# Add and gelu over two 1024x4096 arrays: halves of 64 KB rows become three contiguous blocks of 16, 53 and 59 KB rows

## The chip, the cores and the metric

The kernel runs on one core of a Trainium2 chip. The metric is device time in microseconds (us). Before the change the median of three runs is 120.08 us (120.03 to 120.22). About 0.24 us, 0.2% of that, is what a measurement of this kernel can tell from no change.

## The reference

Two float32 arrays of 1024x4096 go in, one comes out, element by element:

```python
z = x + y
out = 0.5 * z * (1 + np.tanh(np.sqrt(2 / np.pi) * (z + 0.044715 * z ** 3)))
```

Each array has 16.78 MB, so 33.55 MB are read and 16.78 MB written.

## The kernel before

Every array is seen as 128 rows, one for each partition: `xv`, `yv` and `ov` (L87) give partition p the p-th stretch of 32,768 contiguous elements, 128 KB. The kernel works on the two halves of these rows, 64 KB per partition each. The tile `zt` (L117, 128 KB per partition) holds all of x, then z, then the result, in place. The tile `yt` (L118, 64 KB per partition) holds one half of y at a time, so the second half of y can only be loaded when the adds of the first half have read the first.

All transfers are issued by SP, in this order: the first half of y (`load_y`, L128), the first and the second half of x (`load_x`, L123), then the second half of y in two pieces of 12,288 and 4,096 columns (48 and 16 KB per partition), then two stores of 64 KB per partition (`store`, L132). The y piece of 12,288 columns waits for the first six adds, the piece of 4,096 columns for the next two.

VectorE adds in place, `z = z + y`, in pieces of 2,048 columns (`add`, L151; the last two have 1,024). ScalarE follows with the gelu in place (`gelu`, L156). GpSimd takes no part in it (`by_pool` is empty), and no piece goes through PSUM (`in_psum` is empty).

The first store has a wait written by hand (L133 to L139): it isn't issued before add number 8, the first add of the second half, is done (`GATE = 8`).

Two helpers edit the finished program. `begin_early` (L11) moves SP's first two transfers ahead of the barrier at the start. `wait_late` (L23) takes the wait for the last store out of the common end and gives it to ScalarE. A small activation on the tile `one` loads the gelu table while the first loads run (L182, L183).

Of the kernel before, what the change touches and what calls it, by code (L numbers as in the profile page):

```python
# [8 lines left out]
def begin_early(nc, count):  # L9


    head, body = (b.instructions for b in nc.main_func.blocks[:2])
    SP = mybir.EngineType.SP
    moved = [i for i in body if i.engine == SP and isinstance(i, mybir.InstDMACopy)][:count]
    assert not any(i.sync_info and i.sync_info.on_wait for i in moved)
    assert all(i.regs_accessed() == ((), ()) for i in moved)
    at = next(k for k, i in enumerate(head) if i.engine == SP)
    for k, i in enumerate(moved):
        body.remove(i)
        head.insert(at + k, i)  # L20


def wait_late(nc):  # L23

    body, end = (b.instructions for b in nc.main_func.blocks[1:3])
    last = [i for i in body if isinstance(i, mybir.InstDMACopy)][-1]
    (sem,) = [u.id for u in last.sync_info.on_update]
    all_done = end[0]  # L30
    reset = next(i for i in end if isinstance(i, mybir.InstDrain) and i.is_reset_sema)
    at = end.index(reset)
    clear = end[at + 1]
    first, stop = reset.reset_range_start, reset.reset_range_stop
    assert all_done.engine == mybir.EngineType.SP and reset.engine == mybir.EngineType.Pool
    assert isinstance(clear, mybir.InstISA) and clear.engine == mybir.EngineType.Pool
    waits = all_done.sync_info.on_wait
    (its,) = [w for w in waits if w.id == sem]

    end[0] = mybir.InstDrain(  # L40
        name=all_done.name, engine=all_done.engine, debug=all_done.debug, is_reset_sema=False,
        sync_info=mybir.SyncInfo(on_wait=[w for w in waits if w.id != sem], on_update=[]),
    )
    parts = []
    for f, e in ((first, sem), (sem + 1, stop)):
        if f < e:
            nc.gpsimd.sem_clear(range(f, e))
            parts.append(nc.cur_bb.bb.instructions.pop())
    end[at + 1 : at + 2] = parts
    end.append(  # L50
        mybir.InstEventSemaphore(
            name=clear.name, engine=mybir.EngineType.Activation, debug=clear.debug,
            sync_info=mybir.SyncInfo(
                on_wait=[its],
                on_update=[
                    mybir.SyncUpdate(
                        sync_type="semaphore", id=sem, ant_name=its.ant_name,
                        update_mode="sem-sub-imm", update_value=its.wait_value,
                    )
                ],  # L60
            ),
        )
    )


@with_exitstack
def kernel(
    ctx: ExitStack,
    tc: tile.TileContext,
    x: bass.AP,  # L70
    y: bass.AP,
    out: bass.AP,
):

    nc = tc.nc
    P = nc.NUM_PARTITIONS  # L80
    fp32 = mybir.dt.float32
    act = mybir.ActivationFunctionType

    N, D = x.shape
    assert N % P == 0
    TOT = N // P * D
    xv, yv, ov = (a.rearrange("(p n) d -> p (n d)", p=P) for a in (x, y, out))  # L87

    HALF = TOT // 2
    xloads = [HALF, HALF]  # L90
    yloads = [16384, 12288, 4096]
    stores = [16384, 16384]
    chunks = [2048] * 15 + [1024, 1024]
    by_pool = []
    in_psum = []
    GATE = 8

    def ranges(sizes):
        ends = [sum(sizes[: i + 1]) for i in range(len(sizes))]
        assert ends[-1] == TOT  # L100
        return [(e - f, e) for e, f in zip(ends, sizes)]

    xr, yr, sr, cr = (ranges(r) for r in (xloads, yloads, stores, chunks))
    C = len(cr)
    second = next(c for c in range(C) if cr[c][0] == HALF)

    def over(rs, lo, hi):
        return [i for i, (a, b) in enumerate(rs) if a < hi and b > lo]

    pool_sb = ctx.enter_context(tc.tile_pool(name="xz", bufs=1))  # L110
    pool_y = ctx.enter_context(tc.tile_pool(name="y", bufs=1))
    pool_ps = ctx.enter_context(
        tc.tile_pool(name="ps", bufs=max(1, len(in_psum)), space=bass.MemoryType.PSUM)
    )

    one = pool_sb.tile([P, 992], fp32, tag="one", name="one")
    zt = pool_sb.tile([P, TOT], fp32, tag="z", name="z")  # L117
    yt = pool_y.tile([P, HALF], fp32, tag="y", name="y")  # L118
    xp, adds = {}, {}

    def load_x(i):
        a, b = xr[i]
        nc.sync.dma_start(out=zt[:, a:b], in_=xv[:, a:b])  # L123

    def load_y(i):
        a, b = yr[i]
        o = a % HALF
        nc.sync.dma_start(out=yt[:, o : o + b - a], in_=yv[:, a:b])  # L128

    def store(i):  # L130
        a, b = sr[i]
        ins = nc.sync.dma_start(out=ov[:, a:b], in_=zt[:, a:b])  # L132
        if i == 0 and GATE is not None:  # L133
            tc.add_manual_dep(
                ins.ins,
                adds[GATE].name,
                mybir.DependencyInfo(mybir.DependencyClass.Sync, mybir.DependencyReason.DATA),
                reason="the stores join the queue when the last load is nearly done",
            )  # L139

    def to_psum(c):
        a, b = cr[c]
        xp[c] = pool_ps.tile([P, 2048], fp32, tag="xp", name=f"xp{c}")
        nc.scalar.copy(out=xp[c][:, : b - a], in_=zt[:, a:b])

    def add(c):
        a, b = cr[c]
        o = a % HALF
        eng = nc.gpsimd if c in by_pool else nc.vector
        first = xp[c][:, : b - a] if c in in_psum else zt[:, a:b]  # L150
        ins = eng.tensor_add(out=zt[:, a:b], in0=first, in1=yt[:, o : o + b - a])  # L151
        adds[c] = ins.ins

    def gelu(c):
        a, b = cr[c]
        nc.scalar.activation(out=zt[:, a:b], in_=zt[:, a:b], func=act.Gelu_apprx_tanh)  # L156

    sp = [(load_y, i) for i in over(yr, 0, HALF)] + [(load_x, 0), (load_x, 1)]
    sp += [(load_y, i) for i in over(yr, HALF, TOT)]
    sp += [(store, i) for i in range(len(stores))]  # L160
    pool = [(add, c) for c in by_pool]
    dve = [(add, c) for c in range(C) if c not in by_pool]
    order = list(range(second, C))
    acts = [(gelu, c) for c in range(second)] + [(to_psum, c) for c in in_psum]
    acts += [(gelu, c) for c in order]
    assert sorted(order) == list(range(second, C))

    needs = {
        load_x: lambda i: [],
        load_y: lambda i: [(add, c) for c in over(cr, yr[i][0] - HALF, yr[i][1] - HALF)],  # L170
        to_psum: lambda c: [(load_x, i) for i in over(xr, *cr[c])],
        add: lambda c: [(load_x, i) for i in over(xr, *cr[c])]
        + [(load_y, i) for i in over(yr, *cr[c])]
        + [(to_psum, k) for k in in_psum if k == c],
        gelu: lambda c: [(add, c)],
        store: lambda i: [(gelu, c) for c in over(cr, *sr[i])]
        + ([(add, GATE)] if GATE is not None else []),
    }
    queues = [sp, pool, acts, dve]
    done = set()  # L180
    with tc.manual_schedule():
        nc.vector.memset(one[:, :1], 0.0)  # L182
        nc.scalar.activation(out=one[:, :1], in_=one[:, :1], func=act.Gelu_apprx_tanh)  # L183
        while any(queues):
            moved = False
            for q in queues:
                while q and all(n in done for n in needs[q[0][0]](q[0][1])):
                    fn, arg = q.pop(0)
                    fn(arg)
                    done.add((fn, arg))  # L190
                    moved = True
                    if q is not sp:
                        break
            assert moved, [q[:1] for q in queues]

    ctx.close()
    tc.close()
    tc.compile()  # L198
    begin_early(nc, 2)
    wait_late(nc)  # L200
# [30 lines left out]
```

## Time and profile before

| | |
|---|---|
| Median of three runs | 120.08 us (120.03 to 120.22) |
| The profiled execution's own time | 120.19 us |
| Its span, from the first to the last instruction | 118.70 us |
| VectorE busy | 35.5 us, 30% of the span |
| ScalarE busy | 32.0 us, 27% |
| DMA queue of SP | 1008 packets, 50.33 MB, 98.5% of 16 engines' span |

The span is what the profile's views cover; 1.49 us of the profiled execution lie outside it. In the views, a line such as L151 is a line of the kernel, "SPq" is SP's sequencer, which issues the transfers, and a transfer's "landing" is the last of its 16 completion signals. Beside the views, the trace has a record of each DMA packet with its start, its length and its bytes. Here each packet is one partition's row of one transfer (640 of 65,536 bytes, 128 of 49,152 and 128 of 16,384), and each transfer ends with 16 packets of 4 bytes, one on each of the 16 DMA engines. In the view of stretches of time, a packet is counted in the stretch where it starts, so a short stretch can show more than is possible and the next one less.

### The profile page before, as it was taken

The page shows a single profiled execution, that of the slowest core. Times are in us where ns is not written, and L with a number is a line of the kernel's source. Part 1 is how long each engine was busy: PE and PEld are TensorE (multiplying, and loading weights), DVE is VectorE, ACT ScalarE, POOL GpSimd, SP SyncE. Part 2 cuts the span into 40 slices and gives each one's busy share as a digit, 9 for nine tenths or more (in the row PEclk, how much of TensorE's full clock was granted, in tenths as well). Part 3 has the DMA queues.
Part 4 walks back from the last instruction along what each step waited for, and adds up shares of the span by engine and source line. Part 5 has one row for each costly group of instructions (what it writes and reads, how often), then busy time and mean ns, then how long its engine had stood idle before and what let it go on. Part 6 is the DMA issues. An engine that isn't in the chain of part 4 may idle for free.

```text
span 118.7 us, 96 instructions
## 1 busy us (share of the span) xinstructions
DVE 35.5 (30%) x18; ACT 32.0 (27%) x19; POOL 0.2 (0%) x4
## 2 busy tenths in 40 slices
DVE  0000000000000099999900000699999300000000
ACT  5000000000000029899850000079989800000000
POOL 0000000000000000000000000000000000000000
DMA  9889888998899888988898996998899889988890
GB/s 353 353 353 685 375 353 353 596 464 353 353 442 618 353 353 353 685 375 353 353 530 381 414 530 271 431 624 353 353 596 464 353 353 442 618 353 353 353 685 22
DMA packets 1008, 50.33 MB, mean 424 GB/s; under 512 B 112, under 2 KB 112, under 8 KB 112
## 3 DMA queue, kind: packets, MB, share of 16 engines
q1 hardware_dynamic: 1008, 50.33, 98.5%
HBM read 33.55 MB, written 16.78 MB: 424 GB/s over the span
## 4 chain that ended last, share of the span: by engine, by line
DMA 52%; DVE 22%; ACT 2%; DVEq 2%; ACTq 1%; SPq 0%; issue 0%
DMA z<-in_x_dram 34%; DVE z L151 22%; DMA y<-in_y_dram 17%; ACT z L156 2%; DVEq L198 2%; ACTq L198 1%; SPq L128 0%; DVEq L151 0%
## 5 line engine op out<-in xcount | busy, mean ns | idle before, releaser
L151 DVE TENSOR_TENSOR z<-z,y 128x2048 f32<-128x2048 f32 (+1 forms) x17 | 35.5, 2160 | 56.2 <-DMA z<-in_x_dram 40.0
L156 ACT ACTIVATE z<-z 128x2048 f32<-128x2048 f32 (+1 forms) x17 | 30.5, 1807 | 61.3 <-DVE z L151 61.3
L183 ACT ACT_TABLE_LOAD x1 | 1.3, 1283 | 1.3 <-PEq L215 1.3
L182 DVE MEMSET one<- 128x1 f32 x1 | 0.1, 59 | 1.3 <-PEq L215 1.3
L183 ACT ACTIVATE one<-one 128x1 f32<-128x1 f32 x1 | 0.2, 203 | 0.0
L215 POOL MEMSET const-bfloat16-1.0<- 128x1 bf16 x1 | 0.1, 101 | 0.0
L215 POOL MEMSET const-uint8-127<- 128x1 uint8 x1 | 0.1, 101 | 0.0
L215 POOL MEMSET const-float32-0.0<- 128x1 f32 x1 | 0.1, 98 | 0.2 <-issue 0.2
L215 POOL MEMSET const-float32-1.0<- 128x1 f32 x1 | 0.1, 98 | 0.0
## 6 DMA issues: line engine op xcount, KB each, us to landing
y<-in_y_dram SPq DMA_DIRECT2D x1, 6144.0 KB, 20.5
y<-in_y_dram SPq DMA_DIRECT2D x1, 2048.0 KB, 20.9
z<-in_x_dram SPq DMA_DIRECT2D x2, 50.1
out_dram<-z SPq DMA_DIRECT2D x2, 22.9
y<-in_y_dram SPq DMA_DIRECT2D x1, 22.0
```

Source lines behind the costliest of these rows:

```text
L151: ins = eng.tensor_add(out=zt[:, a:b], in0=first, in1=yt[:, o : o + b - a])
L156: nc.scalar.activation(out=zt[:, a:b], in_=zt[:, a:b], func=act.Gelu_apprx_tanh)
L182: nc.vector.memset(one[:, :1], 0.0)
L183: nc.scalar.activation(out=one[:, :1], in_=one[:, :1], func=act.Gelu_apprx_tanh)
L198: tc.compile()
L215: nc = _bacc.Bacc("TRN2", target_bir_lowering=False, num_devices=1)
```

## The change

The arrays are no longer seen as 128 rows of 128 KB. They are taken flat and cut into three blocks that lie one after the other in memory, and each block is cut into 128 rows: block 0 has rows of 4,096 elements (16 KB), block 1 of 13,568 (53 KB), block 2 of 15,104 (59 KB). Row p of a block goes to partition p.

- Loads: y's block 0, y's block 1, x's block 1, y's block 2, x's block 2, x's block 0: six instead of five. Stores: block 1, block 2, block 0: three instead of two.
- y's block 1 is loaded into the place of `zt` where x's block 2 goes later. So x's block 2 waits for all adds of block 1. y's blocks 2 and 0 have a place of their own in `yt`, which grows from 64 to 75 KB per partition.
- Compute: block 1 in pieces of 2,048 columns x6 and 1,280; block 2 in pieces of 2,816 and 2,048 x6; block 0 in two of 2,048.
- The hand-written wait of the first store is on the first add of block 2, the one of 2,816 columns.
- The two helpers stay; the transfers that now go ahead of the barrier are y's block 0 and y's block 1.

```diff
-    xv, yv, ov = (a.rearrange("(p n) d -> p (n d)", p=P) for a in (x, y, out))
+    PIECES = [[2048, 2048], [2048] * 6 + [1280], [2816] + [2048] * 6]
+    LEN = [sum(p) for p in PIECES]
+    GATE = (2, 0)
+    AT = [sum(LEN[:k]) for k in range(3)]
-    HALF = TOT // 2
-    xloads = [HALF, HALF]
-    yloads = [16384, 12288, 4096]
-    stores = [16384, 16384]
-    chunks = [2048] * 15 + [1024, 1024]
-    GATE = 8
+    def rows(a, k):
+        flat = a.rearrange("n d -> (n d)")
+        return flat[P * AT[k] : P * (AT[k] + LEN[k])].rearrange("(p c) -> p c", p=P)
...
+    zt = pool_sb.tile([P, TOT], fp32, tag="z", name="z")
+    yt = pool_sb.tile([P, LEN[2] + LEN[0]], fp32, tag="y", name="y")
+    def z(k, lo=0, hi=None):
+        return zt[:, AT[k] + lo : AT[k] + (LEN[k] if hi is None else hi)]
+    def y_at(k, lo=0, hi=None):
+        hi = LEN[k] if hi is None else hi
+        if k == 1:
+            return z(2, lo, hi)
+        o = 0 if k == 2 else LEN[2]
+        return yt[:, o + lo : o + hi]
+    def load_x(k):
+        nc.sync.dma_start(out=z(k), in_=rows(x, k))
+    def load_y(k):
+        nc.sync.dma_start(out=y_at(k), in_=rows(y, k))
+    def store(k, gate=None):
+        ins = nc.sync.dma_start(out=rows(out, k), in_=z(k))
+        if gate is not None:
+            tc.add_manual_dep(ins.ins, adds[gate].name, ...)
+    def block(k):
+        lo = 0
+        for i, n in enumerate(PIECES[k]):
+            v = z(k, lo, lo + n)
+            adds[k, i] = nc.vector.tensor_add(out=v, in0=v, in1=y_at(k, lo, lo + n)).ins
+            nc.scalar.activation(out=v, in_=v, func=act.Gelu_apprx_tanh)
+            lo += n
...
+        load_y(0)
+        load_y(1)
+        load_x(1)
+        load_y(2)
+        block(1)
+        load_x(2)
+        load_x(0)
+        block(2)
+        store(1, GATE)
+        block(0)
+        store(2)
+        store(0)
```

## The prediction

> **What bounds the kernel now.** I read the page's DMA rows first, then the chain in order of time, the stretches, SP's timeline and the groups by shape.
>
> ```profile
> DMA  9889888998899888988898996998899889988890
> q1 hardware_dynamic: 1008, 50.33, 98.5%
> ```
>
> The transfers fill 98.5% of 16 engines' span. The chain that ended last names VectorE with 22%, yet that isn't the limit: the chain only follows what released what. The stretches (us; DVE, ACT, POOL busy; clock; DMA share; GB/s) show the queue at its full rate in loads and in stores:
>
> ```profile
> 21.70:41.00 19.30, 0.00 (x0) 0.00 (x0) 0.00 (x0) 1.00 1.00 435
> 79.70:99.00 19.30, 13.34 (x8) 13.35 (x8) 0.00 (x0) 1.00 1.00 435
> ```
>
> The packet records say the same engine by engine: each of the 16 chains of packets runs from its first packet to its last without a hole of more than 12 ns. So the span is a start, 116 us of packets and an end, and the change can win only at the start or the end, and lose wherever it leaves the queue empty.
>
> **The packets.** A row takes 2418 ns with 65,536 bytes, 1815 with 49,152 and 611 with 16,384. From the first and last: (2418 - 611) / 3 = 602.3 ns for 16 KB, and 611 - 602.3 = 8.7 ns that each row costs apart from its bytes (check: 3 x 602.3 + 8.7 = 1815.6). The bytes stay. An engine has 8 rows of each transfer; there are 7 transfers now and 9 then, so 16 rows more: 16 x 8.7 = 0.14 us, and two more completion packets of 9 ns: **+0.16 us**. The new rows: 53 KB is 3.3125 x 602.3 + 8.7 = 2004 ns, 8 of them 16.03 us; 59 KB is 2230 ns, 17.84 us; 16 KB is 4.89 us.
>
> [...] The trace has transfers queued behind each other following within 12 ns, so its row decides.
>
> **Compute and the waits.** By shape (busy, mean ns | idle):
>
> ```profile
> L151 DVE TENSOR_TENSOR z<-z,y 128x2048 f32<-128x2048 f32 x15 | 33.2, 2285 | 56.2 <-DMA z<-in_x_dram 40.0 <-DMA y<-in_y_dram 16.2
> L156 ACT ACTIVATE z<-z 128x2048 f32<-128x2048 f32 x15 | 28.6, 1910 | 61.3 <-DVE z L151 61.3
> L151 DVE TENSOR_TENSOR z<-z,y 128x1024 f32<-128x1024 f32 x2 | 2.4, 1219 | 0.0
> L156 ACT ACTIVATE z<-z 128x1024 f32<-128x1024 f32 x2 | 2.0, 1039 | 0.0
> ```
>
> An add of 1,280 columns is then 1219 + 256/1024 x (2285 - 1219) = 1486 ns, one of 2,816 is 2285 + 768/1024 x 1066 = 3085 ns. Adds of 2,048 follow each other every 17.71 / 8 = 2.21 us. The sum of the columns is the same, and the compute lies beside transfers. What counts is SP's **lead** at each wait: how long before the queue runs dry the next transfer is issued.
>
> ```profile
> 0.00 0.38 SPq L128 DMA_DIRECT2D y<-in_y_dram  x1
> 0.43 1.16 SPq L123 DMA_DIRECT2D z<-in_x_dram  x2
> 75.26 17.77 DVE L151 TENSOR_TENSOR z<-z,y 128x2048 f32<-128x2048 f32 x9 [16.19 <-DMA y<-in_y_dram]
> 77.62 17.35 SPq L132 DMA_DIRECT2D out_dram<-z  x2
> ```
>
> The shortest lead now: the store is issued at 77.62 and the engines end the loads at 79.01 (first) to 79.67 (last), 1.39 to 2.05 us, with no hole. The new leads, with today's start (the engine that starts last ends its first row at 4.73, as if begun at 4.73 - 2.42 = 2.31; its last packet is signalled some 0.31 us after its end):
>
> - x's block 2 (waits for all of block 1's adds, and x's block 0 and the stores stand behind it on SP). x's block 1 ends at 2.31 + 4.89 + 16.03 + 16.03 = 39.26, lands at 39.57, adds start 0.10 later (41.27 to 41.37 today), six take 13.31, the small one 1.49: 54.5. y's block 2 ends on the last engine at 39.26 + 17.84 = 57.10, on the first 0.66 earlier, 56.44. Lead 1.9 us: nothing lost.
> - First store (block 2 and block 0's stores stand behind it). The last load has 16 KB rows as today, so the loads end 79.01 - 75.26 = 3.75 to 4.41 us after the add starts, but the gate is 3.09 + 0.08 = 3.17 instead of 2.36 behind it. **Lead 0.58 to 1.24 us**, less than anything the trace shows to be enough.
> - Second store: adds of block 2 take 3.01 + 6 x 2.21 + 0.07 = 16.4 us from 75.35, the last gelu 1.96 more: issued at 93.8. The first store is through on the first engine at 79.1 + 16.03 = 95.1. Lead 1.4, today's 1.39: taken as nothing. The gelu of 2,816 columns, 1910 + 0.75 x 871 = 2.56 us, keeps up with its add.
> - Third store: block 0's gelus end near 98; the second store runs until 113. Nothing.
>
> **The price of the short lead.** The one place where the trace shows a transfer from issue to first packets with an empty queue is the start: issued at 0.00, first packets at 1.01 to 1.79 on the 16 engines. If it is as long at the store, the engine that is last on both sides idles 1.79 - 1.24 = 0.55 us, and its first row may be as much longer than a steady one as at the start (2935 - 2418 = 0.52): 0.55 to 1.07 us. If queued work comes through in 0.58 it is 0. I keep 0 and 1.07 as ends. Between them I take 0 in the forecast, because the lead follows the start, as shown next.
>
> **The start.** It is all there is to win. First packets start at 1.01 to 1.79 (the eighth of 16 at 1.16, the last alone after 1.48), and last 0.40 to 0.94 us longer than the 2418 ns of a steady row. The lag stays: the engine that starts at 1.79 ends last, at 118.31, when the median is near 117.87. The first row now has a quarter of the bytes. Bounds for the last engine: nothing, if both the late start and the 0.52 us are fixed latencies; 0.75 x 0.52 = 0.39 us if the extra goes with the row's length, and 1.79 - 1.01 = 0.78 if no engine starts late: together 1.17. A loss isn't excluded (16 KB rows come due every 0.61 us, a pace that the trace shows only for a transfer queued long before), but it is priced by the same row at 0.5. I take the middle of 0 and 1.17, **-0.58 us**: a start spread about like that of the other 15 engines (4.73 against a median end near 4.28, 0.45) and a third of the extra. With the last engine 0.45 nearer to the others, their leads at the first store grow by as much, 0.58 to 1.03, about the 1.01 of the first packets. So a better start also pays for the gate; a start as today leaves it bare.
>
> [...]
>
> **Sum.** +0.16 (packets) - 0.58 (start) + 0 (waits) = -0.42 us on the profiled execution's 120.19, that is 119.77; it lies 0.11 above the median of 120.08, so 119.66 for the median. The 1.49 us outside the span keep their instructions and are taken as unchanged.
>
> **Rivals**, in the median's frame.
>
> - Start shrinks (forecast): net -0.25 to -1.01, 119.1 to 119.83. For it: the only idle time of the engines is there, the first row is visibly slow, and one engine alone is late. Against it: nothing shows that a late engine depends on row length. Chance 0.42.
> - The first row's extra and the late engine are fixed, and the gate holds: the change does to the time only what its packets cost, 120.08 + 0.16 = 120.24, with a gain of up to 0.4 down to 119.84. For it: in the steady state all rows cost the same per byte. Chance 0.22.
> - The first store's late gate leaves the queue dry near 79 us: +0.16 + 0.55 to 1.07, 120.8 to 121.3; with some gain at the start 120.4. It decides once an engine needs more than its lead, 0.58 to 1.24 us, from issue to packet. For it: 1.01 to 1.79 at the start. Against it: that start is a cold one. Chance 0.32.
> - x's block 2 waits for more than the adds, for instance the gelus of block 1: these end about 1.45 us after the last add (54.5 plus a 1,280 gelu of 1039 + 0.25 x 871 = 1.26 and the wake-ups), lead 0.5 instead of 1.9 and the same price as above. Against it: today the y loads into a read buffer are issued 0.02 us after the sixth add. Chance 0.04.
>
> **Numbers.** Likeliest: 119.66. The forecast's own range is 119.1 to 119.83. Beyond 0.24 us, what a measurement can tell: faster 0.42, within 0.22, slower 0.32 + 0.04 = 0.36. The range 119.3 to 121.0 leaves out the best of the starts (under 0.10) and the dearest of the gaps (under 0.10).
>
> **What would show it.** Packet records: 72 rows on each engine with 611, 2004 and 2230 ns. Start: the last engine's first packet well before 1.79, and the last engine's final packet before 118.2. Gate: the first store issued about 3.17 us after block 2's first add starts, with store packets following the loads within some 12 ns; a hole near 79 us is the third case. x's block 2 issued near 54.5 with no hole near 57. I am wrong altogether if rows of 53 or 59 KB are slower per byte than 27.1 bytes a ns, which nothing here measures for rows that lie side by side: 1% of it would be 1.16 us.

## The result and the profile after

The changed kernel takes 120.70 us (median of four runs, 120.40 to 120.85) against 120.06 (120.00 to 120.22): ratio 1.0048, 95% interval 1.0036 to 1.0060. It is slower by about 0.6 us, where the prediction had it faster by 0.42. The profiled execution took 120.85 us with a span of 119.4, 0.7 longer than before.

One thing is needed to read the later numbers: over all runs, 9 of 24 executions of the changed kernel took 122.4 to 123.0 us, while none of 128 executions of the kernel before was above 121.05; the ratios leave such executions out, so I tell of them by their number.

The queue's rows on the changed kernel's page, and a stretch in the middle of a load (columns as in the prediction: DVE, ACT, POOL busy; clock; DMA share; GB/s):

```profile
DMA  7999898979798978979979977996969697797796
q1 hardware_dynamic: 1296, 50.33, 98.5%
```

```profile
38.50:56.30 17.80, 14.70 (x7) 12.62 (x7) 0.00 (x0) 1.00 1.00 434
```

The share of the queue is the same 98.5%, and the steady rate too: the packet records have rows of 2004 ns (53 KB) and 2229 (59 KB), as the prediction worked out. The share of busy time tells little here: rows that stall count as busy, a row of 2884 ns instead of 2229 with all of its time.

The adds by shape agree with the working to 10 ns:

```profile
L135 DVE TENSOR_TENSOR z<-z,y 128x2816 f32<-128x2816 f32 x1 | 3.1, 3094 | 21.4 <-DMA z<-in_x_dram 21.4
L135 DVE TENSOR_TENSOR z<-z 128x1280 f32<-128x1280 f32 x1 | 1.5, 1484 | 0.0
```

and so does SP's timeline (start, length), with x's block 2 issued at 54.57 (worked out: 54.5) and the first store at 79.05:

```profile
0.00 0.38 SPq L119 DMA_DIRECT2D y<-in_y_dram  x1
...
54.57 0.80 SPq L116 DMA_DIRECT2D z<-in_x_dram  x2
79.05 19.85 SPq L122 DMA_DIRECT2D out_dram<-z  x3
```

So the plan was read rightly; the loss is in what the queue does at three places. I read them from the packet records: the time at which each transfer's last packet is through on the last of the 16 engines. "The last engine" is here, and from here on, the one that is last with the transfer in question; it need not be the same engine for all of them.

| on the last engine, us | before | after | difference |
|---|---|---|---|
| start: end of the first load less 8 steady rows | 2.29 | 2.44 | +0.15 |
| x's block 2: 18.28 instead of the 17.82 that y's block 2 took | | | +0.46 |
| all other packets | 116.01 | 116.08 | +0.07 |
| end of the last packet | 118.31 | 118.98 | +0.68 |

(A first reading, which stands in the expectation of the first run below, gave 0.14 and 0.09 for the start and the packets.) The start did not shrink. At the second place the first rows of x's block 2 took 2385, 2419, 2718 and 2884 ns on four engines instead of 2229; the one with 2718 was nearly last already and became the last. The third place, the hole at the first store, is there as the third case had it, and yet it isn't in the sum. The stretch just before the store's first packets (columns as above):

```profile
79.00:79.90 0.90, 0.90 (x1) 0.88 (x1) 0.00 (x0) 1.00 0.54 224
```

A packet counts where it starts, so the ends of rows begun before 79.00 are not in it; but in the last run below, where the store follows with holes of at most 0.3 us, the same stretch has a share of 2.26 from the rows that start in it:

```profile
79.00:79.90 0.90, 0.90 (x1) 0.90 (x1) 0.00 (x0) 1.00 2.26 965
```

The records of the changed kernel show 15 engines idle for 0.01 to 0.97 us, but the last engine is busy with its loads until 80.31, and the store's packets have been there since 79.90.

### The profile page after: what moved, and what is told of

It reads as the page before. It is cut to its first block, busy times and chain, and to the rows that moved or that the text cites. A ratio compares the mean times of both kernels' runs of the same rounds, so it can differ in the third digit from the quotient of the medians.

```text
span 119.4 us, 101 instructions
## 1 busy us (share of the span) xinstructions
DVE 35.5 (30%) x17; ACT 31.8 (27%) x18; POOL 0.2 (0%) x4
## 3 DMA queue, kind: packets, MB, share of 16 engines
q1 hardware_dynamic: 1296, 50.33, 98.5%
## 4 chain that ended last, share of the span: by engine, by line
DMA 50%; DVE 27%; DVEq 2%; ACT 2%; issue 0%
DMA z<-in_x_dram 50%; DVE z L135 27%; DVEq L157 2%; ACT z L136 2%; DVEq L135 0%
## 5 line engine op out<-in xcount | busy, mean ns | idle before, releaser
L136 ACT ACTIVATE z<-z 128x2048 f32<-128x2048 f32 (+2 forms) x16 | 30.3, 1908 | 65.5 <-DVE z L135 65.4
L135 DVE TENSOR_TENSOR z<-z,y 128x2048 f32<-128x2048 f32 (+1 forms) x9 | 20.7, 2375 | 21.4 <-DMA z<-in_x_dram 21.4
L135 DVE TENSOR_TENSOR z<-z 128x2048 f32<-128x2048 f32 (+1 forms) x7 | 14.7, 2171 | 38.4 <-DMA z<-in_x_dram 38.4
```

Of the source, the lines that this page charges most:

```text
L135: adds[k, i] = nc.vector.tensor_add(out=v, in0=v, in1=y_at(k, lo, lo + n)).ins
L136: nc.scalar.activation(out=v, in_=v, func=act.Gelu_apprx_tanh)
```

## The experiments

Two theories came out of this. **Layout**: first rows that lie one right after the other in memory ("packed") start later. **Lead**: a load that is issued only 1.8 us before the queue runs dry isn't at full rate in time, whatever its rows. Rivals: both are draws of one execution; the stall belongs to the addresses of x's block 2; the late gate of the first store sets the end.

"Start" is from here on the last engine's end of the first load less 8 steady rows, and "lead" is the time from the issue of a load until the first engine runs dry. Times are medians of all executions, with their lowest and highest; the kernel before ran beside them at 120.01 to 120.10.

### The changed kernel again

> The changed kernel unedited, once more. In its first profile the last engine ended 0.68 us later than in the kernel before: 0.14 us of it at the start, 0.09 us in more packets, 0.46 us in x's block 2, whose first rows took up to 2884 ns instead of 2229 on four engines. Theory A (the stall of the first rows of x's block 2 is tied to its wait, and which engines it hits is drawn anew each time): the stall is there again with a maximum between 0.1 and 0.7 us, on other engines, and the time lies in 120.4 to 120.9. Rival B (a single accident of that execution): all first rows of x's block 2 take 2229 to 2240 ns and the time is 120.2 to 120.4.

Measured: 120.47 to 122.95, six of twelve at 120.47 to 121.06 and six at 122.4 and above; the profiled one took 122.65. Its row of x's block 2 (KB, us from issue to landing), and below it that of the first profile:

```profile
z<-in_x_dram SPq DMA_DIRECT2D x1, 7552.0 KB, 22.2
```

```profile
z<-in_x_dram SPq DMA_DIRECT2D x1, 7552.0 KB, 21.2
```

It was issued at 54.82, and on three engines its first packets came at 57.98, 58.13 and 58.43, 3.2 to 3.6 us after the issue, with the engines idle for 1.1 to 1.7 us. That made x's block 2 last 1.40 us longer on the last engine. The adds of block 2 wait for its landing, so the gate opened at 80.25 instead of 79.05, and 13 engines that had ended their loads in time idled 0.55 to 1.84 us. On the last engine x's block 0 then took 0.24 us more than in the first profile and the first store 0.28. Not an accident, then, but the same place with a larger size. The start was 2.69.

> The changed kernel again. Layout theory: last engine's virtual start between 2.4 and 2.9 for the third time. Draw theory: below 2.3 in one of three. Lead theory: either extra time near 57 us of up to 0.7 on some engines (time 120.4 to 121) or packets over 3 us late on a few engines (time above 122).

Measured: 120.80 (120.50 to 122.87, three of eight above 122). In the profile the first rows of x's block 2 are up to 0.35 us late, again on the engine that ends last, whose block took 18.18 instead of 17.81: +0.37. The start was 2.56, the third time above 2.4.

### A longer lead

```diff
-        load_y(0)
         load_y(1)
         load_x(1)
         load_y(2)
+        load_y(0)
```

> y's block 0 is loaded fourth instead of first; nothing else. The adds of block 1 come 4.9 us earlier while x's block 2 is needed at the same time, so its lead grows from 1.9 to about 6.8 us, and the first load has rows of 53 KB. Theory A (the first rows stall because the transfer is issued only 1.9 us before it is needed): no stall, rows of 2229 ns, and the time falls by about 0.46 to 120.2. Rival B (the stall belongs to the rows and addresses of x's block 2): it is there as before, near 57 us, and the time stays above 120.5. On the start: if small first rows make it slower, the last engine's virtual start (end of its first row less a steady row) goes from 2.44 back to about 2.30 and the median from 2.13 to about 1.85; if it's the contiguous layout, it stays.

Measured: 120.83 (120.60 to 121.15), none at 122. x's block 2 was issued at 50.05, 6.3 us before the first engine ran dry. The stall is gone: no first row of x's block 2 over 60 ns late, 17.81 us for the block. So it isn't a matter of its addresses. The time did not fall: the start with 53 KB rows packed 53 KB apart grew to 2.81, which takes back 0.37 of the 0.46. The expectation for the start failed: rows of 53 KB don't start like the 64 KB rows of before, so the length alone isn't what counts.

### A shorter lead in the kernel before

The adds of the first half in another order, so that the y load of 12,288 columns waits for 7.5 adds instead of 6. This is the test from the other side: old rows, old schedule, short lead.

```diff
-    chunks = [2048] * 15 + [1024, 1024]
-    GATE = 8
+    chunks = [2048] * 7 + [1024, 1024] + [2048] * 7 + [1024, 1024]
+    GATE = 9
+    FIRST = [0, 1, 2, 3, 4, 6, 7, 5, 8]
...
-    dve = [(add, c) for c in range(C) if c not in by_pool]
+    dve = [(add, c) for c in FIRST + list(range(second, C))]
...
-    acts = [(gelu, c) for c in range(second)] + [(to_psum, c) for c in in_psum]
+    acts = [(gelu, c) for c in FIRST] + [(to_psum, c) for c in in_psum]
```

> The kernel before with the adds of its first half in another order, so that the y load of 12,288 columns waits for 7.5 adds instead of 6: issued at about 58.0 instead of 54.7, lead 1.6 us on the first engine instead of 4.9; rows 128 KB apart, all else the same. Theory A (a load needs about as long a lead as at the start, 1.6 to 2.8 us): first rows of that load stall by 0.1 to 0.7 us on some engines, time 120.1 to 120.6. Rival L2 (only contiguous blocks stall): no stall, 120.05 within 0.1.

Measured: eight executions at 119.95 to 120.41 and four at 121.98 to 122.39, which the kernel before never shows. SP's timeline of the profiled one, which took 121.98:

```profile
57.82 1.46 SPq L129 DMA_DIRECT2D y<-in_y_dram  x2
79.08 17.35 SPq L133 DMA_DIRECT2D out_dram<-z  x2
```

The lead is 59.64 - 57.82 = 1.82 us. On two engines the load's first packets came at 60.87 and 61.03, 3.05 and 3.21 us after the issue, the engines had idled 1.1 and 1.4 us, and the first rows took 0.6 and 0.9 us more. The load lasted 16.18 us instead of 14.50 on the last engine. So a short lead makes the second group of executions without packed rows too. It doesn't show the 0.46: the eight other executions have the kernel before's own time (median 120.05), and none of them was profiled. Whether a smaller stall at this lead needs packed rows is therefore open.

### The gate of the first store

```diff
-    GATE = (2, 0)
+    GATE = (1, 6)
```

> The changed kernel with the first store's wait on the last add of block 1 instead of the first add of block 2, so that it joins the queue near 55 us behind x's block 0. Theory C (the holes near 79.9 us on 15 engines cost nothing, because the last engine has none): holes gone, time as the changed kernel's within 0.15 us. Rival D (the late gate sets the end): faster by 0.3 to 0.6. A third possibility is that the early store slows the loads, which would show as longer rows before 80 us and a slower time.

Measured: 123.38 (121.08 to 123.89), five of six above 122. The third possibility of the expectation came true. The first of the three stores is now issued at 56.26 instead of 79.05:

```profile
56.26 42.29 SPq L122 DMA_DIRECT2D out_dram<-z  x3
```

I took it a second time for another profile:

> The changed kernel with the first store in the queue behind x's block 0, again. If the store queued behind the loads is what stretches them: rows of x's block 0 longer by 0.1 to 0.7 us near 79 us again, and in an execution above 122 either longer stretches there or packets of x's block 2 over 3 us late, near 58 us. No idle gap before the store's first rows.

Measured: 122.17 (121.18 to 123.56), two of four above 122; the profiled executions are at 121.08 and 121.22. No engine idles at the store in either. But the rows of the last load, x's block 0, which now have the store right behind them, take 0.1 to 0.7 us longer, and the load takes 5.55 us on the last engine in both profiles instead of 4.86. In the second profile:

```profile
78.70:79.80 1.10, 1.10 (x2) 1.00 (x1) 0.00 (x0) 1.00 0.88 238
```

Rows that start in the stretch fill 0.88 of it, but carry 238 GB/s; at the steady rate above (1.00 with 434) it would be 382.

So the hole of the late gate is not what the changed kernel loses by, and an early store costs 0.69. Of this kernel's executions above 122 there is no profile, and where they lose more stays open.

### The layout alone

```diff
-        flat = a.rearrange("n d -> (n d)")
-        return flat[P * AT[k] : P * (AT[k] + LEN[k])].rearrange("(p c) -> p c", p=P)
+        return a.rearrange("(p n) d -> p (n d)", p=P)[:, AT[k] : AT[k] + LEN[k]]
```

> The changed kernel's blocks, order and waits, but each block is a range of columns of the old view, so that the rows lie 128 KB apart again. Theory L (contiguous blocks make the start slower, whatever the first row's length): the last engine's virtual start falls from 2.4-2.8 us to about 1.95, as with small first rows in the kernel before, and the best executions come down to 119.95-120.05; the stall at x's block 2 stays (same lead). Rival R (the start is drawn at random, or depends on what else the schedule issues): the start stays at 2.4 or above and the best executions near 120.4.

Measured: 120.21 (120.08 to 120.97), ratio 1.0019 (1.0005 to 1.0033). The start is 1.99, as the layout theory has it. The first load's landing (KB, us) in the changed kernel and in this one:

```profile
y<-in_y_dram SPq DMA_DIRECT2D x1, 2048.0 KB, 7.7
```

```profile
y<-in_y_dram SPq DMA_DIRECT2D x1, 2048.0 KB, 7.2
```

The stall shrank to one first row 0.19 us late and two under 0.1. The expectation had it stay; afterwards the reason is plain: with the last engine nearer to the others, x's block 1 lands earlier against the first engine, so the lead is 2.18 instead of 1.78.

The other way round, the kernel before with contiguous halves:

```diff
-    xv, yv, ov = (a.rearrange("(p n) d -> p (n d)", p=P) for a in (x, y, out))
+    def half(t, a, b):
+        h = a // HALF
+        flat = t.rearrange("n d -> (n d)")
+        rows = flat[P * HALF * h : P * HALF * (h + 1)].rearrange("(p c) -> p c", p=P)
+        return rows[:, a - HALF * h : b - HALF * h]
...
-        nc.sync.dma_start(out=zt[:, a:b], in_=xv[:, a:b])
+        nc.sync.dma_start(out=zt[:, a:b], in_=half(x, a, b))
...
```

The y loads and the stores are changed in the same way.

> The kernel before with its halves taken from the flat arrays, so that each half is contiguous and its rows lie 64 KB apart instead of 128 KB; schedule and waits as before. Theory L: the last engine's virtual start grows from 2.30 to 2.4-2.8, time 120.2 to 120.6. Rival R: start near 2.3, time 120.05 within 0.1.

Measured: 120.14 (119.95 to 120.36), ratio 1.0005 (0.9995 to 1.0015), start 2.26. The layout theory misses here: halves whose 64 KB rows are packed start like the kernel before.

### Small first rows

```diff
-    yloads = [16384, 12288, 4096]
+    yloads = [4096, 12288, 12288, 4096]
```

> The kernel before with its first y half in two loads, 16 KB rows first and 48 KB rows second; layout, waits and stores as before. Rows per engine +8, so +0.08 us by the packets. If small first rows make the start slower: the median engine's virtual start goes from 1.85 to about 2.13, and the time to 120.3. If the start doesn't depend on the row: 120.15. If small first rows shorten it, as the prediction had it: 119.6.

> The kernel before with 16 KB rows in its first load, again. Layout and row length: virtual start about 1.95 to 2.1 and a time 0.1 us under the kernel before's, as the first time. Draw theory: start as likely above 2.3 as below, and no difference in time.

Measured: 119.94 (119.77 to 120.75) and 119.97 (119.88 to 120.30), ratios 0.9987 (0.9971 to 1.0003) and 0.9994 (0.9982 to 1.0005); starts 1.95 and 1.87. So small first rows do shorten the start, by some 0.1 to 0.4 us against 2.08 to 2.29, if they lie 128 KB apart. The gain in time is at most 0.1 us, within what can be told from none.

The kernel before, unedited:

> The kernel before again. Layout theory: last engine's virtual start 2.1 to 2.4 as in its first profile (2.30), 120.05. Draw theory: anything from 1.9 to 2.9.

Measured: 120.02 (119.90 to 120.68), start 2.10.

```diff
-    yloads = [16384, 12288, 4096]
+    yloads = [2048, 14336, 12288, 4096]
```

> The kernel before with its first y half in loads of 8 and 56 KB rows (the run with 16 and 48 KB rows gave 119.94 and a last engine's virtual start of 1.97 instead of 2.30). If the start shrinks with the first row's length: about 1.9, time 119.9. If the first rows drain before the second transfer is ready (8 rows of 8 KB last 2.5 us, and the second is issued at 0.43): holes near 3 us and no gain, 120.0 to 120.3.

Measured: 119.95 (119.88 to 120.25), ratio 0.9984 (0.9970 to 0.9998), start 2.13, no holes near 3 us: no gain beyond that of 16 KB rows.

The contiguous halves of `half` above, with `yloads = [4096, 12288, 12288, 4096]`:

> The kernel before on contiguous halves (rows 64 KB apart) with 16 KB of each row loaded first. If the first rows start late only when they are packed without a space between them (16 KB rows 16 KB apart): virtual start 1.9 to 2.1, time about 119.95. If it is their distance, shorter is later: 2.2 to 2.4, time 120.1 to 120.3.

Measured: 119.96 (119.89 to 120.30), start 2.07: the first case. Small rows 64 KB apart start nearly as early as 128 KB apart (1.87 to 1.99).

### Other sizes, and both causes mended

```diff
-    PIECES = [[2048, 2048], [2048] * 6 + [1280], [2816] + [2048] * 6]
+    PIECES = [[2048, 1024], [2048] * 6 + [1280], [2816] + [2048] * 6 + [1024]]
```

> The changed kernel with blocks of 12, 53 and 63 KB rows: y's block 2 lasts 1.2 us longer, so the lead of x's block 2 grows from about 1.8 to about 3.0 us; layout contiguous, order the same. Theory A (the lead): stalls of first rows gone or under 0.1 us in the profile, and the executions above 121.5 become rare; with the start unchanged the time is 120.2 to 120.5. Rival B (rows and addresses of x's block 2): stalls of 0.2 us and more near 58 us again, and executions above 122 in about half of the runs.

Measured: 121.76 (121.66 to 121.87). The lead was 2.90 and x's block 2 lost nothing on the last engine, but I had overlooked that the last load became shorter by 1.2 us, while the gate stayed 3.2 us behind the adds' start:

```profile
79.95:80.75 0.80, 0.80 (x1) 0.80 (x1) 0.00 (x0) 1.00 0.00 0
```

The store was issued at 79.94, when all engines had been through by 79.89; its packets came 0.85 to 1.00 us later, and the first store's step on the last engine took 17.14 us instead of 16.01: 1.13. This is the wait of the prediction's third case (priced there at 0.55 to 1.07), measured where it holds: with a lead of zero on the last engine.

The same sizes with rows 128 KB apart:

> Both at once: rows 128 KB apart and blocks of 12, 53 and 63 KB, so a lead of 3.0 us. If layout at the start and lead at x's block 2 are the two causes, both are gone and only the packets are left: last engine's virtual start about 1.95, no stall, 119.95 to 120.1, no executions above 121. If something else in the changed schedule costs time, it stays above 120.3.

Measured: 121.28 (121.24 to 121.37), with the same loss of 1.13 at the first store; start 2.06, no stall.

Then the gate's piece made smaller, with packed rows and with rows 128 KB apart:

```diff
-    PIECES = [[2048, 1024], [2048] * 6 + [1280], [2816] + [2048] * 6 + [1024]]
+    PIECES = [[2048, 1024], [2048] * 6 + [1280], [1792] + [2048] * 7]
```

> The contiguous blocks of 12, 53 and 63 KB rows again (lead of x's block 2 about 3.0 us), now with a first add of 1,792 columns in block 2, so that the first store comes 2.1 us behind the start of block 2's adds instead of 3.2 and the last engine's lead is 1.0 us instead of 0. If the hole near 80 us was all that made the kernel with the longer lead slow: 121.76 - 1.13 = 120.6. Theory A: no first row near 57 us over 0.3 us late, and no executions above 121.5. Rival: executions near 122.6 again.

> The same with rows 128 KB apart: start about 2.0 us on the last engine, no stall, no hole on the last engine; 121.28 - 1.13 = 120.15, and 119.95 to 120.2 in all executions. If it stays at 120.4 or above, something besides layout, lead and gate costs time in three blocks.

Measured: 121.90 (121.60 to 122.04) and 121.46 (121.24 to 121.50). The last engine has no hole at the first store any more, but 63 KB rows make block 2's compute longer, and now the second store comes late. In the first of the two it is issued at 96.36, and the first engine had run dry at 95.96:

```profile
95.00:97.20 2.20, 2.20 (x2) 1.91 (x2) 0.00 (x0) 1.00 0.00 0
```

On the last engine the second store takes 20.35 and 20.24 us instead of 19.05: +1.3 and +1.2. These four runs say less than they were meant to; what they do say is that three waits of this schedule (x's block 2, the first and the second store) have under 2 us to spare. The clean test keeps the sizes:

```diff
-        flat = a.rearrange("n d -> (n d)")
-        return flat[P * AT[k] : P * (AT[k] + LEN[k])].rearrange("(p c) -> p c", p=P)
+        return a.rearrange("(p n) d -> p (n d)", p=P)[:, AT[k] : AT[k] + LEN[k]]
...
-        load_y(0)
         load_y(1)
         load_x(1)
         load_y(2)
+        load_y(0)
```

> The changed kernel with rows 128 KB apart and y's block 0 loaded fourth: lead of x's block 2 about 6.8 us, first load with 53 KB rows in the old view. If layout and lead are the whole loss: last engine's virtual start 2.0 to 2.3, no stall near 57 us, the last engine without a hole near 80 us, time 120.0 to 120.2 with none above 121. If something else in the three blocks costs time: above 120.4.

Measured: 120.16 (120.08 to 120.33), ratio 1.0005 (0.9993 to 1.0016), start 2.14, x's block 2 in 17.82 on the last engine. SP's timeline shows the lead, 56.33 - 49.37 = 7.0 us:

```profile
49.37 0.82 SPq L115 DMA_DIRECT2D z<-in_x_dram  x2
78.41 19.85 SPq L121 DMA_DIRECT2D out_dram<-z  x3
```

With both mended the loss is gone but for about 0.1, what the packets cost. Against the same order with packed rows (120.83, start 2.81) the layout is worth 0.67 us of time and 0.67 of start. In the time alone the layout is nearly everything: with rows 128 KB apart and y's block 0 first, the lead is 2.18 and the time already 120.21. That the short lead costs its 0.46 rests on the packet records: the stall is there in three profiles of the changed kernel, and gone with packed rows at a lead of 6.3. The first load of 6,784 KB landed after 19.2 us with packed rows and after 18.5 with rows 128 KB apart:

```profile
z<-in_y_dram SPq DMA_DIRECT2D x1, 6784.0 KB, 19.2
```

```profile
z<-in_y_dram SPq DMA_DIRECT2D x1, 6784.0 KB, 18.5
```

### All profiles together

Start, from one profile each:

| first rows, distance | start of the last engine, us |
|---|---|
| 64 KB, 128 KB apart | 2.29, 2.10, 2.08 |
| 53, 16, 12 and 8 KB, 128 KB apart | 2.14; 1.99, 1.95, 1.87; 2.06, 1.92; 2.13 |
| 64 and 16 KB, 64 KB apart | 2.26; 2.07 |
| 16 KB, packed | 2.44, 2.69, 2.41, 2.56, 2.54 |
| 12 KB and 53 KB, packed | 2.46, 2.66; 2.81 |

No value of the last two rows is below 2.41 and none of the others above 2.29, and each of the four chips on which these runs were made shows both sorts, so it is neither a draw nor one chip against another. Packing as such isn't the cause: the 64 KB rows 64 KB apart are packed too and start at 2.26. Why distances of 12, 16 and 53 KB start late and 64 and 128 KB don't is open: no run separates a distance under 64 KB from one that isn't a multiple of 64 KB.

Lead of the load that waits for the adds, and what its first rows did:

| lead, us | first rows |
|---|---|
| 1.60, 1.82 | idle 1.1 to 1.7 on two or three engines (executions at 122) |
| 1.66, 1.67, 1.78 | up to 0.35, 0.20 and 0.66 late |
| 2.08, 2.18 | under 0.06; 0.19 late |
| 2.7 to 3.5 (four runs with 63 KB rows) | up to 0.31 late; the last engine's block at most 0.2 longer |
| 4.9 and more | under 0.1 late |

## Why the prediction was wrong

The measured 120.70 lies within the range of 119.3 to 121.0, but on the other side of before than the forecast. Two of the sum's steps failed. In the profile the forecast was -0.42 and the result +0.68; of the 1.10 between them the start makes 0.73 and the wait 0.46, and the packets give 0.09 back. That the range held the time is luck: its upper end stood there for a gap at the first store, which cost nothing.

**The start, "-0.58 us", was +0.15.** The step took the late last engine and the long first row as things that go with the row's length, and the layout as something that only the steady rate could show. Length does help: 1.87 to 1.99 with 16 KB rows 128 KB apart, against 2.08 to 2.29 with 64 KB, about 0.2 of the 0.58. Laying the same rows 16 KB apart takes it back and more: 2.41 to 2.69. The prediction named the layout only as a risk to the rate of the new rows, and that rate held (2004 and 2229 ns); it priced a loss at the start by the rows' length, and never asked what their distance does to the one part of the run where engines do wait. Its "against it" (nothing shows that a late engine depends on row length) was a fair doubt.

**"Lead 1.9 us: nothing lost" cost 0.46 us, and 1.4 in the executions at 122.** The lead was worked out well (1.78 measured). The fault is the yardstick: 1.39 us had been enough for a store, and I held a load against it. Where engines waited for the first store here, its first packets came 0.84 to 1.00 us after the issue and at once at nearly full rate (2034 to 2049 ns instead of 2004). A load has no such record before, except the start, where the same trace shows 1.6 to 2.3 us until an engine is at full rate. The prediction used that row for the store, which came sooner, and not for the load, whose first rows were up to 0.66 us late. The fourth rival had a wait at the right place for the wrong reason: x's block 2 was issued at 54.57, as the adds alone allow.

**The packets, +0.16, were +0.07**: right in kind, half the size, since rows follow one another a little faster than their records last (eight of 16 KB take 4.86 us, not 4.89).

**The first store** was the rival given 0.32, and its view came true to the tenth: issue 3.16 us behind the adds' start, holes on 15 engines. It cost nothing because it decides on the last engine alone, and that had 80.31 - 79.05 = 1.26 us, more than the 0.84 to 1.00 that the store took; the prediction had reckoned with up to 1.79. Only with no lead at all, in the run with 63 KB rows, did it cost its 1.13. The forecast's time is wrong not by this but by the two steps above.

At the distances here the steady rate is the same (a 53 KB row takes 2004 ns packed and 128 KB apart), and contiguous small rows start later, at 2.41 to 2.81 us against 1.87 to 2.29.

## What to carry to other kernels

When one queue is full from end to end, look at each wait on it for its lead, and hold it against the same kind of transfer: here a store needed about 1.0 us, while first rows of a load were up to 0.66 us late at a lead of 1.8, up to 0.31 at 2.7 to 3.5 and under 0.1 from 4.9 on; and a short lead can show as a part of the executions that are 2 us slower, so one execution doesn't tell. Changing how rows lie in memory may leave the steady rate as it is and still move the start (here 2.81 us against 2.14, with 2004 ns a row in both), so take the first row from the packet records, not only the rate. And in a schedule where several waits have under 2 us to spare, changing one size moves the next wait: my mended sizes lost more than the change did, in all four runs.

## What the runs showed of the hardware

- At the start, from issue to full rate (end of the first load less 8 steady rows), a load took 1.4 to 2.8 us, engine by engine, and in some executions the first packets of a load issued in mid-run came only 3.05 to 3.6 us after the issue on two or three of 16 engines; in others of the same kernel all engines went on without a gap, the first of them 1.8 us after the issue. What makes the difference is open. Where an engine waited for packets, none came earlier than 0.84 us after the issue.
- A store queued right behind a load stretched the load's last rows: 5.55 us instead of 4.86 for 16 KB per partition, in two profiles of two. In the kernel before such a store was issued 1.39 us before the first engine ended its loads, and the load's rows were not stretched (4.86 us).
- Rows 12, 16 or 53 KB apart began 0.1 to 0.9 us later on the last engine than rows 64 or 128 KB apart (2.41 to 2.81 us against 1.87 to 2.29), at the same steady rate (2004 ns for a row of 53 KB at distances of 53 and of 128 KB).
